# Two-layer hybrid step in float32 on one core: seven products for the latent gate and up projections, and a feed-forward cut in two phases through DRAM

## The chip, the cores and the metric

The kernel runs on one core of one Trainium2 chip (trn2). The metric is the device time of one execution in microseconds; the time of a kernel is the median of its runs. Beside the runs there is one profiled execution, whose records give the rows below. Engines are named as the profile does: PE is TensorE's matmul, PEld its weight load, DVE is VectorE, ACT is ScalarE, POOL is GpSimd, SP is SyncE, which issues the DMAs.

## The reference, cut to what matters

Two trunk layers run over 1024 latent tokens and 256 context tokens with a model width of 1024 and a feed-forward width of 2816. Each layer is a modulated norm, one input projection, three mixers (long convolution, short convolution, attention), an output projection with a gated residual, and then the feed-forward:

```python
x = x + g1 * (y @ P['w_out'][l])
h2 = rmsnorm(x, P['g_norm2'][l]) * (1 + sc2) + sh2
ff = (jax.nn.silu(h2 @ P['w_ff_gate'][l]) * (h2 @ P['w_ff_up'][l])) @ P['w_ff_down'][l]
x = x + g2 * ff
```

`sc2`, `sh2`, `g1` and `g2` are vectors of the width 1024 from a modulation that differs between latent and context tokens. Everything is float32.

## The kernel before

**Products.** Tokens lie along the columns in three chunks (`CH`): two of 512 latent tokens, `ci` 0 and 1, and one of 256 context tokens, `ci` 2. Every float32 operand is held as two float32r parts, hi (a copy on ACT, line 325) and lo (value minus hi, on DVE or POOL, line 326), and each product is three matmuls: hi·hi, hi·lo, lo·hi (`mm3`, line 335). A tile of 128 outputs over the width 1024 is a group of 24 matmuls in one of the eight PSUM banks: three of them belong to the pool `pa`, five to `pb`, given out in turn.

**The feed-forward** (`ffn`, line 1380) goes over 22 tiles f of 128 hidden columns. For each f it loads the gate and up weights (1024 words a partition each), splits them into hi and lo, and `gu` does for the chunks 2, 0, 1 a gate and an up group. ACT puts Silu over the gate (line 1394), DVE multiplies by up from PSUM (1395), POOL splits the product into hi and lo in a ring of two (`ze`, 1396 and 1397). Then `down` takes the hidden tile of the f before: for each chunk and each of 8 output tiles three matmuls, after which DVE adds the result, times g2, to the residual x in SBUF (1411). The last `down` takes two tiles at once, so six matmuls to a group; in layer 1 it also writes the result out (1416). The residual x and both norms' results stay in SBUF all the time.

**What lies ahead of it.** `out_proj` (line 1354) runs over chunk 0, then chunk 1; context went before, inside attention. DVE adds to x (1368), ACT squares (470), POOL sums the squares (473). From the sum `bcast_rstd` makes the reciprocal root: PE (485), a chain of small DVE operations (487, 349 to 356, 494), PE (498). `norm_mod` (504) then scales the eight k tiles on DVE (517), and makes hi and lo: half of the tiles by ACT and DVE (524, 525), half by ACT and POOL (520 to 522). The norm of a chunk is put off by a number of ticks (`soon`, `tick`); that of chunk 1 is made while PE is at the feed-forward's first groups.

**Beside it in layer 0** run the modulation vectors of layer 1: `mod_tiles` (385), three tiles of 1024 words for each f, all through one buffer `rawm`: DMA, DVE (399), POOL (395), ACT (396), then the next tile's DMA.

**Order.** Each engine works through its own queue in order. A planner makes that order when the kernel is built: by program order as priority, taking a later instruction first where its own clock says that the earlier one still waits. A `Mem` object gives every buffer its place in SBUF by the span of program order in which it lives, so two buffers may share a place, and the later one then waits for the readers of the earlier. `open_z` and `close_z` lay out a region anew: `zw` (eight weight buffers) and `ze` during the feed-forward.

## Time and profile before

| | |
|---|---|
| median of 3 runs | 3739.16 us (3738.04 to 3741.91) |
| the profiled execution, its own time | 3742.36 us |
| its span from first to last instruction | 3740.5 us |
| PE busy | 3540.3 us (95%) |
| DVE, POOL, ACT busy | 2226.4 us (60%), 1260.5 us (34%), 1085.3 us (29%) |
| mean granted clock of TensorE | 0.962 |

The page of the profile gives the busy time of each engine, and the span in 40 slices. Matmuls overlap, so a busy PE isn't PE at its peak: how fast it goes is read from how many matmuls it does in a stretch. The chain of waits follows the work back from the last instruction; a piece of it with a count, such as "PE pa L335 x72", is so many matmuls one behind the other, and its time by its count is the pace of one. Granted clock is that of TensorE, 1.00 being 2.4 GHz and 0.5 being 1.2 GHz.

### The profile page before, as it was taken

What the parts mean: (1) busy time and instruction counts of PE and PEld (TensorE: products, weight loads), DVE (VectorE), ACT (ScalarE), POOL (GpSimd) and SP (SyncE); (2) the same over time, 40 slices, a digit from 0 to 9 for tenths busy, and PEclk for the clock granted to TensorE, in tenths of its full rate; (3) what the DMA queues carried; (4) which work ended last, traced back from release to release, by engine and by line L of the source; (5) the groups of instructions that cost most, each with busy time, mean ns of one, the idle gap of its engine ahead of it and who ended that gap; (6) DMA issues with size and microseconds to landing.
All of it is one profiled execution on the core that took longest, in us unless ns stands there. A gap on an engine that the chain in (4) does not pass through costs nothing.

```text
span 3740.5 us, 45633 instructions
## 1 busy us (share of the span) xinstructions
PE 3540.3 (95%) x17792; PEld 2811.7 (75%) x17792; DVE 2226.4 (60%) x3420; ACT 1085.3 (29%) x1955; POOL 1260.5 (34%) x1063
## 2 busy tenths in 40 slices
PE   7899889998999999999999988999899999999999
PEld 4488865555788888888887886655578888888888
DVE  4657577766565666566458757767655445444543
ACT  4422344544331211121124234444533110111010
POOL 3412346665443323332132234556542111111110
PEclk9799889998999999999999999899899999999999
DMA  7611100013322222221122110001331111111111
GB/s 278 230 61 60 38 15 17 21 41 110 103 73 74 79 68 85 74 79 51 46 73 66 62 40 13 11 13 33 117 103 52 34 40 35 46 35 40 34 46 63
DMA packets 84005, 239.23 MB, mean 64 GB/s; under 512 B 8491, under 2 KB 20779, under 8 KB 80588
## 3 DMA queue, kind: packets, MB, share of 16 engines
q1 hardware_dynamic: 83788, 236.30, 19.2%
q8 instruction: 140, 2.29, 0.3%
q14 instruction: 77, 0.63, 0.1%
HBM read 207.89 MB, written 28.38 MB: 63 GB/s over the span
## 4 chain that ended last, share of the span: by engine, by line
PE 81%; DVE 11%; issue 2%; POOL 2%; ACT 2%; DMA 2%; SPq 0%; DVEq 0%; POOLq 0%; ACTq 0%
PE pb L335 40%; PE pa L335 26%; PE st L335 5%; PE y L1166 3%; PE pa L1108 2%; DVE arena L463 1%; PE pa L498 1%; PE pa L1127 1%; DVE arena L741 1%; DVE arena L742 1%; DMA zm<-in_w_modk 1%; PE pa L1110 1%; DVE arena L355 1%; DVE arena L354 1%; POOL arena L1184 1%
## 5 line engine op out<-in xcount | busy, mean ns | idle before, releaser
L335 PE MATMUL pb<-operands,zw 128*128 128x512 f32 (+1 forms) x5592 | 1114.0, 359 | 14.6 <-ACT zw L325 7.3
L335 PEld LDWEIGHTS pb<-operands,zw 128*128 128x128 f32 x5592 | 939.2, 190 | 170.7 <-ACT zw L325 8.1
L335 PE MATMUL pa<-operands,zw 128*128 128x512 f32 (+1 forms) x3240 | 646.7, 359 | 0.2 <-POOL operands L522 0.2
L335 PEld LDWEIGHTS pa<-operands,zw 128*128 128x128 f32 x3240 | 544.3, 189 | 91.8 <-issue 1.2
L325 ACT CAST zw<-arena 128x1024 fp32r<-128x1024 f32 x190 | 199.3, 1050 | 1069.9 <-PE pb L335 571.9
L1396 POOL TENSOR_SCALAR ze<-arena 128x256 fp32r<-128x256 f32 (+1 forms) x132 | 74.9, 568 | 1084.9 <-DVE arena L1395 1084.9
L326 DVE TENSOR_TENSOR zw<-arena,zw 128x1024 fp32r<-128x1024 f32 x174 | 254.9, 1485 | 271.1 <-ACT zw L325 266.8
L335 PE MATMUL pb<-ze,zw 128*128 128x512 f32 (+1 forms) x1980 | 411.7, 358 | 0.0
L1411 DVE SCALAR_TENSOR_TENSOR arena<-pb,arena 128x512 f32<-128x512 f32 (+1 forms) x630 | 386.4, 659 | 11.1 <-PE pb L335 11.1
L335 PEld LDWEIGHTS pb<-ze,zw 128*128 128x128 f32 x1980 | 333.1, 188 | 62.4
L1184 POOL TENSOR_TENSOR arena<-pt,arena 128x512 f32<-128x512 f32 x256 | 338.4, 1322 | 88.0 <-ACT pt L1181 75.2
L335 PE MATMUL st<-operands 97*128 97x512 f32 (+1 forms) x1056 | 326.5, 414 | 7.5 <-ACT pt L1181 7.5
L335 PEld LDWEIGHTS st<-operands 97*128 97x128 f32 x1056 | 193.0, 199 | 109.7 <-issue 68.4
L1181 ACT ACTIVATE pt<-st 128x512 f32<-128x512 f32 (+1 forms) x352 | 201.6, 578 | 227.9 <-PE st L335 216.9
L1395 DVE TENSOR_TENSOR arena<-arena,pb 128x512 f32<-128x512 f32 (+1 forms) x83 | 49.5, 597 | 351.3 <-PE pb L335 344.4
L335 PE MATMUL pa<-ze,zw 128*128 128x512 f32 (+1 forms) x1188 | 254.8, 357 | 0.0
L1411 DVE SCALAR_TENSOR_TENSOR arena<-pa,arena 128x512 f32<-128x512 f32 (+1 forms) x378 | 234.7, 659 | 7.1 <-PE pa L335 7.1
L395 POOL TENSOR_TENSOR arena<-arena 128x1024 f32<-128x1024 f32 x48 | 130.6, 2721 | 296.8 <-DVE arena L399 296.8
L335 PEld LDWEIGHTS pa<-ze,zw 128*128 128x128 f32 x1188 | 200.8, 188 | 37.3
L1166 PE MATMUL y<-pt,kv 128*64 128x512 f32 (+1 forms) x704 | 194.1, 621 | 1.5 <-ACT pt L1181 1.5
L1109 DVE TENSOR_REDUCE arena<-pa 128x1 f32<-128x512 f32 x256 | 168.4, 686 | 36.1 <-PE pa L1108 31.6
L1397 POOL TENSOR_TENSOR ze<-arena,ze 128x256 fp32r<-128x256 f32 (+1 forms) x132 | 148.4, 1124 | 10.9
(240 smaller groups left out, 3992.4 us busy)
## 6 DMA issues: line engine op xcount, KB each, us to landing
zm<-in_w_modk SPq DMA_DIRECT2D x24, 1024.0 KB, 6.3
arena<-in_w_out SPq DMA_DIRECT2D x48, 512.0 KB, 3.5
arena<-in_w_mod SPq DMA_DIRECT2D x48, 512.0 KB, 3.4
arena<-in_w_g SPq DMA_DIRECT2D x44, 512.0 KB, 3.5
arena<-in_w_u SPq DMA_DIRECT2D x44, 512.0 KB, 3.5
arena<-in_w_dn SPq DMA_DIRECT2D x44, 512.0 KB, 4.3
arena<-in_w_in SPq DMA_DIRECT2D x24, 512.0 KB, 3.5
yd<-arena SPq DMA_DIRECT2D x14, 640.0 KB, 3.3
```

The source lines that it names most:

```text
L325: nc.scalar.copy(hi.r, raw.f)
L326: (e or nc.vector).tensor_tensor(out=lo.r, in0=raw.f, in1=hi.f, op=ALU.subtract)
L335: self.nc.tensor.matmul(out, a, b, start=(j == 0), stop=(j == n - 1))
L395: nc.gpsimd.tensor_tensor(out=w.f, in0=w.f, in1=c, op=ALU.mult)
L1108: nc.tensor.matmul(p, q, kh[:96, 512 * c:512 * c + 512], start=True, stop=True)
L1109: v.reduce_max(out=mx[:, t, c:c + 1], in_=p, axis=AX.X)
L1166: ins = nc.tensor.matmul(y[64 * e:64 * e + 64, :n], G["kv"][:, kt0 + k + e, h, 0:64], pts[k + e].f[:, :n], start=(k == 0), stop=(k == nkt ...
L1181: ex = nc.scalar.activation(pt.f[:, :n], st[:, :n], AF.Exp)
L1184: (v if k in KDV else gp).tensor_tensor(out=acc.f[:, :n], in0=pt.f[:, :n], in1=(acc if k > 1 else pts[0]).f[:, :n], op=ALU.add)
L1396: nc.gpsimd.tensor_scalar(out=hi, in0=sg.f, scalar1=1.0, scalar2=0.0, op0=ALU.mult, op1=ALU.add)
L1397: nc.gpsimd.tensor_tensor(out=lo, in0=sg.f, in1=hids[f].f[:, s:s + n], op=ALU.subtract)
L1411: nc.vector.scalar_tensor_tensor(out=xx, in0=p[:, :n], scalar=g2[:, m, q:q + 1], in1=xx, op0=ALU.mult, op1=ALU.add)
```

## The change

For latent tokens the product of a pair of f tiles (256 outputs), the width 1024 and 1024 tokens is seen as 2x2 blocks: A of 128 x 512 weights, B of 512 x 512 activations. Seven block products of 12 matmuls each (4 k tiles, three matmuls) take the place of eight. Sums and differences of weight blocks (S1 to S4) are made on POOL for every pair, those of activation blocks (T1 to T4) once a layer, on DVE and POOL. Part of the additions of results is done by accumulating on in the same PSUM bank after it was read (`mma` with `add`), the rest by DVE. Context tokens keep their plain product (`context`).

The feed-forward is two phases: `gate_up` for all pairs, which writes the hidden values to DRAM (`hd`), then `down`, which reads them back two tiles at a time, splits them, and does six matmuls to a group. The residual x is written to DRAM (`xd`) by `out_proj` and read back when `down` begins. All of norm 2 of chunk 1, and the T forms, are made by `rest` after `out_proj`. The SBUF region of the kernel grows (`NW`, `NZ`), the reserve for software DMA descriptors shrinks (`SCRATCH`). In layer 0 the modulation tiles come five to a pair.

```diff
-NW = 53184
-NSMALL = 960
+NW = 57024
+SCRATCH = 1024
+NSMALL = 736
-NZ = 13312
+NZ = 16896
...
+    def mma(self, out, ops, add):
+        n, j = 3 * len(ops), 0
+        for ah, alo, bh, bl in ops:
+            for a, b in ((ah, bh), (ah, bl), (alo, bh)):
+                self.nc.tensor.matmul(out, a, b, start=(j == 0 and not add), stop=(j == n - 1), skip_group_check=add)
                 j += 1
...
+    def shifted(self, l, k, u):
+        nc = self.nc
+        sh = self.mod[l].v(2)[:, 24 + k, 0:1]
+        hi, lo = self.form(), self.form()
+        nc.scalar.activation(hi.r, u, AF.Identity, bias=sh)
+        nc.vector.scalar_tensor_tensor(out=lo.r, in0=u, scalar=sh, in1=hi.f, op0=ALU.add, op1=ALU.subtract)
+        return hi, lo
+    def forms_first(self, l, us):
+        return {"11": [self.shifted(l, k, us[k]) for k in range(4)], "21": [self.shifted(l, k, us[k]) for k in range(4, 8)]}
...
+    def forms_rest(self, l, u1, u2):
...
+        def split(name, k, t, e):
+            hi, lo = self.form(), self.form()
+            nc.scalar.copy(hi.r, t)
+            e.tensor_tensor(out=lo.r, in0=t, in1=hi.f, op=ALU.subtract)
+            F[name][k] = hi, lo
+        for k in range(4):
+            t2 = self.t5()
+            gp.tensor_tensor(out=u1[k], in0=u2[k], in1=u1[k], op=ALU.subtract)
+            v.scalar_tensor_tensor(out=t2.f, in0=u2[4 + k], scalar=sh[:, 4 + k:5 + k], in1=u1[k], op0=ALU.add,
+                                   op1=ALU.subtract)
+            split("T2", k, t2.f, gp)
+            v.scalar_tensor_tensor(out=u1[4 + k], in0=u1[4 + k], scalar=sh[:, 4 + k:5 + k], in1=t2.f, op0=ALU.add,
+                                   op1=ALU.subtract)
+            t2.free()
+        for k in range(4):
+            split("T1", k, u1[k], v)
+            v.scalar_tensor_tensor(out=u2[k], in0=u2[4 + k], scalar=d[:, k:k + 1], in1=u2[k], op0=ALU.add,
+                                   op1=ALU.subtract)
+        for k in range(4):
+            split("T3", k, u2[k], gp)
+        for k in range(4):
+            F["22"][k] = self.shifted(l, 4 + k, u2[4 + k])
+        for k in range(4):
+            split("T4", k, u1[4 + k], gp)
...
 (out_proj)
+                if m % 2:
+                    nc.sync.dma_start(self.xd[:, m - 1:m + 1, t0:t0 + n],
+                                      x[ci].f[:, n * (m - 1):n * (m + 1)].rearrange("p (k n) -> p k n", n=n))
...
+    def gate_up(self, l, cx, F, rest, extra, ahead):
+        ring = Ring(self.zq, 1024)
+        names = ("11", "12", "S2", "S1", "S3", "21", "22", "S4")
...
+        def prepare():
+            j, w, n = todo.pop(0)
+            src = block(j, w, n)
+            f = ring.get()
+            nc.scalar.copy(f.r[:, 0:512], src)
+            v.tensor_tensor(out=f.r[:, 512:1024], in0=src, in1=f.f[:, 0:512], op=ALU.subtract)
...
+        def free(j, w, *ns):
+            for n in ns:
+                have.pop((j, w, n)).free()
+            need(j, w)
...
+        def result(w, name, src, add=None):
+            B = state["hid"]
+            if w == "g":
+                B[name] = o = self.rings["hb"].get()
+                if add is not None:
+                    v.tensor_tensor(out=o.f, in0=src, in1=add, op=ALU.add)
+                    src = o.f
+                nc.scalar.activation(o.f, src, AF.Silu)
+            elif add is not None:
+                t = self.t5()
+                v.tensor_tensor(out=t.f, in0=src, in1=add, op=ALU.add)
+                gp.tensor_tensor(out=B[name].f, in0=B[name].f, in1=t.f, op=ALU.mult)
+                t.free()
+            else:
+                v.tensor_tensor(out=B[name].f, in0=B[name].f, in1=src, op=ALU.mult)
+        def first(j, w):
+            st = state[w] = dict(X=self.ps(), E=None)
+            (a11,) = need(j, w, "11")
+            self.mma(st["X"], ops(a11, F["11"]), False)
+            st["p1"] = self.t5()
+            nc.scalar.copy(st["p1"].f, st["X"])
+            st["E"] = self.ps()
+            a11, a12 = need(j, w, "11", "12")
+            context(j, w, 0, a11, a12)
+            free(j, w, "11")
+            self.mma(st["X"], ops(a12, F["21"]), True)
+            free(j, w, "12")
+            result(w, "11", st["X"])
+        def second(j, w):
+            st = state[w]
+            p1, Y, Z = st["p1"], self.ps(), self.ps()
+            (f,) = need(j, w, "S2")
+            self.mma(Y, ops(f, F["T2"]), False)
+            free(j, w, "S2")
+            a, b = self.t5(), self.t5()
+            v.tensor_tensor(out=a.f, in0=Y, in1=p1.f, op=ALU.add)
+            (f,) = need(j, w, "S1")
+            self.mma(Z, ops(f, F["T1"]), False)
+            free(j, w, "S1")
+            (f,) = need(j, w, "S3")
+            self.mma(Y, ops(f, F["T3"]), True)
+            free(j, w, "S3")
+            v.tensor_tensor(out=b.f, in0=Y, in1=p1.f, op=ALU.add)
+            a21, a22 = need(j, w, "21", "22")
+            context(j, w, 1, a21, a22)
+            free(j, w, "21")
+            result(w, "c", st["E"])
+            result(w, "22", Z, b.f)
+            b.free()
+            (f,) = need(j, w, "S4")
+            self.mma(Z, ops(f, F["22"]), True)
+            free(j, w, "S4")
+            result(w, "12", Z, a.f)
+            a.free()
+            self.mma(Y, ops(a22, F["T4"]), True)
+            free(j, w, "22")
+            result(w, "21", Y, p1.f)
...
+            if j == 0:
+                need(0, "g")
+                rest()
+                first(0, "g")
+                first(0, "u")
+                second(0, "g")
+                second(0, "u")
+            else:
+                for w in "gu":
+                    first(j, w)
+                    if (j, w) == sets[-1]:
+                        ahead()
+                    second(j, w)
...
+                    nc.sync.dma_start(self.hd[l][:, 2 * j + q, 512 * t:512 * t + 512], b.f)
...
+    def hid_split(self, f):
+        raw = self.hraw.pop(f)
+        for q in range(2):
+            h = self.hids[f + q] = self.rings["hid"].get()
+            for s, n in ((0, 512), (512, 768)):
+                src = raw.f[:, T * q + s:T * q + s + n]
+                self.nc.scalar.copy(h.r[:, s:s + n], src)
+                self.nc.gpsimd.tensor_tensor(out=h.r[:, T + s:T + s + n], in0=src, in1=h.f[:, s:s + n], op=ALU.subtract)
+    def down(self, l, x, early, done):
+        ws = [self.load_split(r, 1024) for r in early]
+        self.hid_load(l, 2)
+        for ci, (s, n) in enumerate(CH):
+            x[ci] = self.al(KD * n)
+            for m in range(0, KD, 2):
+                nc.sync.dma_start(x[ci].f[:, n * m:n * m + 2 * n].rearrange("p (k n) -> p k n", n=n),
+                                  self.xd[:, m:m + 2, s:s + n])
+        for f0 in range(0, NF, 2):
...
+            def ahead():
+                for a, b in F.pop("11") + F.pop("21"):
...
+                self.hid_load(l, 0)
+                self.hid_split(0)
```

`zq`, the ring of weight forms, has five buffers: a product that is done frees one, and the hi and lo of the form five places on are made in it.

## Rows read from the trace of the kernel before

**Rows 1.** Windows: stretch, length; PE, PEld, DVE, ACT, POOL busy; granted clock; DMA.

```profile
1110.00:1900.00 790.00, 790.00 (x4099) 676.77 (x4098) 462.71 (x669) 138.66 (x206) 219.52 (x160) 1.00 0.21 68
2890.00:3730.00 840.00, 840.00 (x4339) 718.56 (x4338) 388.41 (x592) 90.11 (x118) 99.69 (x120) 1.00 0.12 40
```

**Rows 2.** The chain of waits in the feed-forward: start, us, what.

```profile
1203.83 16.32 PE pa L335 x72
...
1400.74 22.10 PE pb L335 x120
...
1429.69 3.50 PE pb L335 x15
...
1567.25 22.10 PE pb L335 x120
...
3717.61 7.00 PE pb L335 x30
```

**Rows 3.** Groups by shape, layer 1's feed-forward (count, busy us, mean ns, idle before).

```profile
L326 DVE TENSOR_TENSOR zw<-arena,zw 128x1024 fp32r<-128x1024 f32 x59 | 70.3, 1220 | 106.1 <-ACT zw L325 106.1
...
L1395 DVE TENSOR_TENSOR arena<-arena,pb 128x512 f32<-128x512 f32 x29 | 20.0, 688 | 205.0 <-PE pb L335 201.2 <-PE pa L335 3.7
...
L325 ACT CAST zw<-arena 128x1024 fp32r<-128x1024 f32 x58 | 61.1, 1054 | 526.7 <-PE pb L335 296.8 <-PE pa L335 155.9 <-issue 74.0
...
L1394 ACT ACTIVATE arena<-pb 128x512 f32<-128x512 f32 x20 | 11.9, 594 | 79.6 <-PE pb L335 79.6
L1397 POOL TENSOR_TENSOR ze<-arena,ze 128x512 fp32r<-128x512 f32 x39 | 50.7, 1300 | 3.3
```

**Rows 4.** The same of layer 0, where modulation tiles run beside.

```profile
L326 DVE TENSOR_TENSOR zw<-arena,zw 128x1024 fp32r<-128x1024 f32 x57 | 103.4, 1841 | 84.1 <-ACT zw L325 84.1
...
L399 DVE SCALAR_TENSOR_TENSOR arena<-arena 128x1024 bf16<-128x1024 f32 x46 | 56.2, 1222 | 84.4 <-DMA arena<-in_w_mod 54.7 <-POOL ze L1397 29.7
...
L395 POOL TENSOR_TENSOR arena<-arena 128x1024 f32<-128x1024 f32 x46 | 124.9, 2715 | 288.2 <-DVE arena L399 288.2
```

**Rows 5.** DVE in order of time, layer 0 (start, us; idle before in brackets).

```profile
1407.64 0.42 DVE L1395 TENSOR_TENSOR arena<-arena,pb 128x256 f32<-128x256 f32 x1
1411.17 1.22 DVE L399 SCALAR_TENSOR_TENSOR arena<-arena 128x1024 bf16<-128x1024 f32 x1 [3.11 <-DMA arena<-in_w_mod]
```

**Rows 6.** Order of time ahead of the feed-forward of layer 1: DVE, ACT, POOL.

```profile
2818.16 0.74 DVE L1368 SCALAR_TENSOR_TENSOR arena<-pb,arena 128x512 f32<-128x512 f32 x1
...
2840.52 0.16 DVE L487 TENSOR_SCALAR arena<-pa 128x4 f32<-128x4 f32 x1
...
2844.29 0.69 DVE L494 TENSOR_TENSOR arena<-arena 128x512 f32<-128x512 f32 x1
2846.28 2.07 DVE L517 SCALAR_TENSOR_TENSOR arena<-arena,pa 128x512 f32<-128x512 f32 x3 [1.30 <-PE pa L498]
2848.26 0.74 DVE L525 SCALAR_TENSOR_TENSOR operands<-arena,operands 128x512 fp32r<-128x512 f32 x1
...
2849.76 1.26 DVE L525 SCALAR_TENSOR_TENSOR operands<-arena,operands 128x512 fp32r<-128x512 f32 x1
...
2819.14 1.28 ACT L1394 ACT_TABLE_LOAD   x1 [0.61 <-PE pb L335]
...
2849.18 1.29 POOL L522 TENSOR_TENSOR operands<-arena,operands 128x512 fp32r<-128x512 f32 x1 [6.60 <-ACT operands L521]
```

**Rows 7.** PE's waits, 1000 to 1100 us; a window as in rows 1.

```profile
PE pb L335 <- POOL operands L522: 1.0, 1, 1.0
PE pa L498 <- DVE arena L494: 0.8, 1, 0.8
...
1016.00:1028.00 12.00, 6.74 (x31) 5.44 (x30) 8.73 (x17) 3.77 (x5) 3.57 (x2) 0.72 0.30 89
```

**Rows 8.** DMAs by kind: count, KB each, us to landing.

```profile
arena<-xd SPq DMA_DIRECT2D x16, 256.0 KB, 3.1
...
arena<-in_xT SPq DMA_DIRECT2D x1, 1024.0 KB, 5.6
```

More of the change, by code (lines that the diff above doesn't have):

```diff
@@ L202, in grow, with shrink @@
         self.count = len(self.bufs)
+    def shrink(self, keep):
+        ks = [k for k in range(self.count) if self.busy[k]]
+        for k in range(self.count):
+            if k not in ks:
+                self.bufs[k].free()
+        self.bufs = [self.bufs[k] for k in ks]
+        for t in keep:
+            t.k = ks.index(t.k)
+        self.busy, self.count, self.at = [True] * len(ks), len(ks), 0
     def close(self):
@@ L372, in consts @@
         self.xd = self.dram.tile([P, KD, T], F32, name="xd")
+        self.hd = [self.dram.tile([P, NF, T], F32, name=f"hd{l}") for l in range(DEPTH)]
         self.kd = [[self.dram.tile([P, 8, 512], F32, name=f"kd{l}{c}") for c in range(2)] for l in range(DEPTH)]
@@ L528, in norm_mod, with norm_raw @@
         return hi, lo
+    def norm_raw(self, l, ci, x, acc):
+        n = CH[ci][1]
+        (r,) = self.bcast_rstd([(acc, 1.0 / D)], n)
+        acc.free()
+        a = self.am[l].f[:, 16:32].rearrange("p (a b) -> p a b", b=2)
+        us = [x[:, k, :] for k in range(KD)]
+        for k in range(KD):
+            self.nc.vector.scalar_tensor_tensor(out=us[k], in0=us[k], scalar=a[:, k, 0:1], in1=r[:, :n], op0=ALU.mult,
+                                                op1=ALU.mult)
+        return us
@@ L1401, in down @@
-        def down(fs, done=None):
-            ws = [self.load_split(self.i["w_dn"][l, f], 1024) for f in fs]
-            for ci in LAST if done and l + 1 < DEPTH else range(3):
+        hids = self.hids
+        ws = [self.load_split(r, 1024) for r in early]
[5 more added lines that the diff above has]
+                                  self.xd[:, m:m + 2, s:s + n])
@@ L1404, in down @@
+        for f0 in range(0, NF, 2):
+            fs, last = (f0, f0 + 1), f0 == NF - 2
+            nws = None
+            for ci in LAST if last and l + 1 < DEPTH else range(3):
                 (s, n), acc = CH[ci], None
@@ L1418, in down @@
                     self.tick()
-                if done:
+                    if ci == 0 and m == 1 and not last:
+                        self.hid_split(f0 + 2)
+                        nws = [self.load_split(self.i["w_dn"][l, f], 1024) for f in (f0 + 2, f0 + 3)]
+                        if f0 + 4 < NF:
+                            self.hid_load(l, f0 + 4)
+                if last:
                     done(ci, acc)
@@ L1551, in run, with rest @@
                 early = ()
-                for ci in cis:
-                    self.soon(NDLY[ci], norm2, ci)
-            self.close_rings("w")
-            self.rings["w"] = Ring(self.zw[4:] + self.zw[:4], 1024)
-            self.rings["hid"] = Ring(self.ze, 2 * T)
+                if cis == (0,):
+                    self.soon(NDLY[0], norm2, 0)
+            self.close_rings("w", "raw")
+            for part in "ab":
+                self.close_z(part)
+                self.open_z(part, "forms")
+            self.fplaces = self.zf + self.zg
+            self.open_rings(raw=("f", 1024, 4), sw=("f", 512, 4))
+            assert not self.late
+            def rest():
+                norm2(1)
+                F.update(self.forms_rest(l, h2[0], h2[1]))
+                x[0].free()
+                x[1].free()
+                self.open_rings(hb=("f", 512, 8))
             extra = None
@@ L1573, in extra @@
                         self.close_rings("rawm")
+            def ahead():
+                for a, b in F.pop("11") + F.pop("21"):
+                    a.free()
+                    b.free()
+                self.open_rings(hrr=("f", 2560, 1), hdr=("r", 2560, 2))
+                self.rings["hid"] = Ring(self.rings["hdr"].bufs, 2 * T)
+                self.rings["hr"] = Ring(self.rings["hrr"].bufs, 2560)
+                self.hraw, self.hids = {}, {}
+                self.hid_load(l, 0)
+                self.hid_split(0)
+            self.gate_up(l, h2[2], F, rest, extra, ahead)
+            early = [self.fetch(self.i["w_dn"][l, f]) for f in range(2)]
+            for hl in (*F.values(), list(zip(*h2[2]))):
+                for a, b in hl:
+                    a.free()
+                    b.free()
+            self.close_rings("sw", "hb")
+            for part in "ab":
+                self.close_z(part)
+            for part in "ab":
+                self.open_z(part, "operands")
+            self.rings["raw"].shrink(early)
+            self.rings["w"] = Ring(self.zw, 1024)
+            self.rings["hid"].grow(self.ze)
+            self.rings["hr"].grow(self.zh)
             def norm1(ci, acc, l=l, h=h):
@@ L1587, in run @@
             self.filler = None
-            self.ffn(l, h2, x, done, extra)
-            self.close_rings("hid", "w")
+            self.down(l, x, early, done)
+            self.close_rings("hrr", "hdr", "w")
+            for name in ("hid", "hr"):
+                self.rings.pop(name)
         self.close_rings("raw", "t5")
```

152 lines of the change are left out of this document (100 added, 52 removed).

## The prediction

> **What bounds the kernel now.** First the windows over the feed-forward of each layer: PE is busy in all of 790.00 and 840.00 us, at a granted clock of 1.00, which is 2.4 GHz, while DVE has 462.71 and 388.41, POOL 219.52 and 99.69, ACT less [rows 1]. A busy PE proves little, so next its pace, from the chain of waits, which in these stretches is nothing but matmuls. 72 matmuls of 512 columns take 16.32 us: 226.7 ns each. The piece of 120 holds 48 of 256 columns beside 72 of 512, so (22.10 - 16.32) / 48 = 120.4 ns. In `down` 15 of 512 columns take 3.50 us, 233.3 ns, and 30 of them in the last `down`, with six to a group and DVE idle half the time, 7.00 us: the same, so DVE doesn't set that pace [rows 2]. The same piece comes again after 1567.25 - 1400.74 = 166.51 us for four tiles f, 41.63 us each [rows 2]. By the paces gate and up take 96 x 226.7 ns + 48 x 120.4 ns = 27.5 us of it, and the rest, 14.1 us, is `down`. There is no slack: the feed-forward, 22 x 41.63 = 916 us in each of two layers, is as long as its matmuls, and one taken out is a gain of its full pace as long as nothing else comes late.
>
> **What is removed.** For a pair of tiles and one of the two weights the latent chunks take 2 x 2 x 24 = 96 matmuls of 512 columns; seven products of 12 are 84. 12 x 226.7 ns = 2.72 us, times 11 pairs, 2 weights and 2 layers (44 sets): **119.7 us** less. Context keeps its 48 matmuls, `down` its count. A set is then 84 x 226.7 + 48 x 120.4 ns = 24.8 us of PE, a pair 49.6.
> *A price from the Trainium skill.* The page TensorE: Matmul & The Clock Gate, section Back-to-back issue gap, gives some 131 ns as the sustained spacing of 512-column matmuls; by it the removed work would be worth 528 x 131 ns = 69 us, and the forecast some 50 us worse. The trace has 226.7 ns here, at full clock [rows 2], so the measurement decides.
>
> **Do the other engines still fit?** Per pair: DVE makes 16 lo parts of 512 words, which I put at half of a 1024 one, 0.61 us as in layer 1 to 0.92 as in layer 0 [rows 3, 4], and 12 additions or multiplications of 0.69 [rows 3]: 18 to 23 us. POOL has 8 weight sums and 3 products at 1.30 [rows 3]: 14.3. ACT has 16 copies at half of 1.05, two of p1 and five Silu of 0.59 [rows 3]: 12.6. Layer 0 adds five modulation tiles: DVE 6.1, POOL 13.6 [rows 4]. All stay under 60% of 49.6. DVE's evictions in `down` halve in number, which gains nothing, as PE's pace there was its own [rows 2].
>
> **Start of the phase.** Before, norm 2 of chunk 1 was hidden by 33 us of context and chunk-0 groups; what PE waited there was 1.0 and 0.8 us in layer 0 [rows 7]. Now PE has only `first` of gate and up ready, 2 x 24 x (226.7 + 120.4) ns = 16.7 us, and then needs T2. In layer 1 PE leaves `out_proj` near 2816.2 (the first context group, 2.9 us, releases ACT at 2819.14), and the last eviction starts at 2818.16, behind norm 2 of chunk 0 [rows 6]. That norm now has eight lo parts on DVE, not four: 4 x 0.74 later, so x is done at 2821.9. Square and sum at ACT's and POOL's prices (0.59 and 1.30 [rows 3]) and PE's reduction give 2824.7; DVE's root chain 4.5 (2840.52 to 2844.98), PE and its hand-over 1.3, eight scalings of 0.66 as 2.07 / 3 shows them with their overlap, 5.3 [rows 6]: 2835.8. T2 is eight DVE operations and four lo parts on POOL. Side by side that is 8 x 0.74 plus 1.9 for the last copy and lo, 7.8; taking turns, 8 x 0.74 + 4 x 1.29 = 11.1 [rows 6]. So T2 ends between 2843.6 and 2846.9; PE would take its last k tile at 2835 or so. A stall of 8 to 11 us, 3 to 5 more for T1, on which DVE spends another 5.9 while PE has 2.7 of work. After a gap the clock is below full for a while: 0.72 over 12 us with some 5 of idle [rows 7]; I add 2.5. Less the 1.5 of before: **+14 a layer, 28 in all**; from 10 (DVE frees x early, as the 1.26 and 0.74 of the same operation show that turns vary [rows 6]) to 44 (all of DVE's and POOL's part in turns).
> The writes of x in `out_proj` are 8 DMAs on SP for the two latent chunks, and 4 for context; each stands ahead of weight fetches on SP's queue and waits for an eviction that PE has just fed. I take 0, at most 5 a layer.
>
> **The seam to `down`.** The first hidden pair is loaded and split inside the last `second`, 16.5 us of PE: a load of 1.3 MB, 5.6 us for 1 MB [rows 8], then four copies and four lo parts, some 6.5 us of POOL [rows 3]. x lies where `hb` lay, whose last slot goes free after an addition, a product and a write: 0.69 + 1.30 [rows 3] + about 3.1, then 3.1 to read x [rows 8], 8.2 us after PE's last product. PE goes on meanwhile through eight banks of 6 x 233.3 ns, 11.2 us: hidden. **+2 a layer, 4 in all** (0 to 20, if the bulk of x, 12 DMAs, comes slower).
>
> **Inside the phase** a set has two narrow places. Y may be added to by S3·T3 only after DVE has read it for `a`, with S1·T1, 2.72 us, as cover. Z may be added to by S4·B22 only after DVE made `b` and the result 22; cover is the context product, 2.89 us. In it DVE has 0.69 + 0.69 and one lo of 0.61 to 0.92: 2.0 to 2.3 us. Where a lo, whose two inputs lie in SBUF, meets POOL, both are longer: a 1024 lo takes 1.22 us in layer 1, and 1.84 in layer 0 with its modulation tiles on POOL [rows 3, 4].
> *The rule of the Trainium skill,* SBUF — State Buffer, section Who interferes with whom: a two-input DVE operation and a POOL operation that reads SBUF lock each other out for a whole instruction. By that a lo could lose a whole 1.30 us more, the stretch would take 3.6 of 2.9 us, and a meeting in every set would cost 44 x 0.7 = 31 us in place of the 12 below; the 1.84 is a mean over meetings and misses, so the rows speak for some loss but not for this size.
> In layer 0 before, with POOL busy 219.52 of 790 us, 28% [rows 1], a lo of 512 words was thus 0.31 longer. In layer 1 POOL will be as busy (14.3 of 49.6): 2.0 + 0.31 still fits, so only odd cases wait, and I take 0.15 us a set, **+3** (0 to 15). In layer 0 it is twice as busy, a lo 0.6 longer and the stretch at its limit: 0.4 us a set, +9; and DVE's queue stands at modulation tiles that came late, 84.4 us over 46 of them, 1.8 each [rows 4], with groups of the feed-forward behind. Before, nothing was urgent behind it. Now a block of w = 3 us (wait and work) that falls ahead of one of the two reads costs on average w²/2 for each place in 24.8 us: 0.36 us, times 48, 17; I take half, as PE gives way once and is then late itself. **+18** for layer 0 (4 to 45).
> The pace of the new products may be that of `down`, where operands lie in a z region: 23 of 56 moving parts lie there, so up to 1518 x 6.7 ns = +10; hidden tiles moved the other way give up to -7. I take +1.
>
> **The sum**, against the profiled execution's own 3742.4: -119.7 + 28 + 4 + 3 + 18 + 1 = -65.7, so 3676.7. The median of the runs lies 3.2 lower than that execution: **3675**, rounded up.
>
> **The rivals.**
> *All is hidden.* Start and seams cost their lower ends, 10 + 0 + 0 + 4 - 7 = 7: 3739 - 113 = 3626, with scatter up to 3645. For it speaks the planner, which fills gaps; against it that T2 stands behind a chain of a length that rows 6 give. Chance 0.13.
> *DVE's queue paces the sets (slower).* In program order the copy and lo for the buffer freed by the context product stand ahead of result 22. They can't begin before that product ends; in that order PE would wait 0.53 + 0.61 (copy, lo), 0.69 for 22, in the up set 0.69 more for the context result, and hand-overs: some 2.4 us in each of 44 sets, 106 us. With start and seam: -119.7 + 106 + 54 = +40, **3780**. It decides the sign from (119.7 - 54) / 44 = 1.5 us a set on. Against it: the order isn't the program's. DVE takes line 1395 of the next tile ahead of a modulation tile, L399, that program order has first [rows 5]; result 22 is ready during the context product and would be taken first. But the planner's clock is not the chip's: the same row shows DVE then standing 3.11 us. Chance 0.12.
> *The change doesn't make products cheaper than what it puts around them.* If the stall at the start, the seam and layer 0 all come out at their upper ends, 44 + 20 + 45 + 10, and layer 1 near its middle, 125 meets 119.7: no change, 3739 to 3745. Chance 0.05.
>
> **How the numbers follow.** Forecast 0.70 (within 3645 to 3725), rivals 0.13, 0.12, 0.05. What differs by under 0.2%, 7.5 us, a measurement of this kernel can't tell from no change. Faster: 0.70 + 0.13 = 0.83; same 0.05; slower 0.12. The range goes from 3630 to 3730: it leaves out a quarter of the first rival, 0.03, and the two others, 0.17, which makes 0.2; the lower bound of the sum, 3626, and the upper ends of all costs together, some 3755, lie just outside.
>
> **What would show it.** Right: a set of 24.8 us in layer 1 with no PE wait over 1 us; between `out_proj` and the first T2 product a PE gap of 8 to 16 us on DVE or POOL of `forms_rest`, with the clock below 1.00 after it; the gap at the seam under 3 us; layer 0's sets longer than layer 1's by some 0.7 us. Wrong: matmuls of the new products off 226.7 ns; PE waits on DVE's reads of Z or Y in every set; a gap at the seam on the DMA of x or of `hd`; a longer stretch outside the feed-forward, which would mean that the new places in SBUF cost something.

## The result and the profile after

The changed kernel takes **3798.57 us** (median of 4 runs, 3794.74 to 3804.2), the kernel before 3740.36 beside it: a ratio of 1.0157, 95% interval 1.014 to 1.0175. It is slower by 58 us, where 65 us of gain were forecast. The profiled execution's span is 3796.3 us; before it was 3740.5. Divided at the ends of the matmuls of `out_proj` and `down`:

| stretch | before, us | after, us | difference |
|---|---|---|---|
| up to the feed-forward of layer 0 | 1037.7 | 1041.8 | +4.1 |
| feed-forward, layer 0 | 921.2 | 1003.4 | **+82.2** |
| from there to the feed-forward of layer 1 | 857.3 | 859.4 | +2.1 |
| feed-forward, layer 1 | 924.3 | 891.7 | **-32.6** |

One change, two layers, two signs. The windows of the kernel after (columns as in [rows 1]) are `gate_up` and `down` of layer 0, then those of layer 1:

```profile
1041.80:1734.45 692.65, 598.52 (x2915) 494.66 (x2914) 339.38 (x454) 214.88 (x377) 334.72 (x186) 0.94 0.31 100
1734.45:2045.20 310.75, 308.06 (x1591) 262.05 (x1590) 207.24 (x310) 60.53 (x89) 93.19 (x58) 1.00 0.26 92
2904.60:3484.00 579.40, 566.62 (x2915) 479.23 (x2914) 257.71 (x349) 170.75 (x279) 190.91 (x138) 0.98 0.23 75
3484.00:3796.30 312.30, 306.77 (x1585) 261.38 (x1583) 201.03 (x287) 47.00 (x60) 76.86 (x41) 1.00 0.27 95
```

`down` is alike in both layers. The two `gate_up` phases hold the same 2915 matmuls, yet layer 0's is 113.25 us longer: 81.35 us in which PE stands (692.65 - 598.52 against 579.40 - 566.62), and 31.9 us in which the same matmuls take longer, at a granted clock of 0.94 instead of 0.98. The other engines are far from full: ACT, the least loaded, works 31% of layer 0's phase, DVE 49%, POOL 48%.

What sets layer 0 apart is the 48 modulation tiles. PE's longest waits from 1125 to 1770 us, 79.2 us with the two left out (line waited for; us, times, longest):

```profile
PE pa L361 <- ACT arena L423: 41.7, 9, 5.4
PE pb L361 <- DVE arena L1588: 18.7, 17, 3.0
PE pa L361 <- ACT arena L1572: 11.1, 8, 1.5
PE pb L361 <- DVE arena L1595: 3.2, 1, 3.2
```

L423 is the sum that ACT makes for a modulation tile, L1588 the sum `a`, L1595 `b`, L1572 the copy of P1. PE reads nothing that L423 writes; one of the nine waits in order of time shows what it stood for. First PE, then DVE, then ACT (start, us; in brackets the idle time before and what ended it):

```profile
1191.89 2.98 PE L361 MATMUL pb<-operands,zq 128*128 128x256 f32 x24
1200.23 5.46 PE L361 MATMUL pa<-operands,zq 128*128 128x512 f32 x12 [5.36 <-ACT arena L423]
1205.48 3.10 PE L361 MATMUL pb<-operands,zq 128*128 128x512 f32 x12
...
1195.28 1.23 DVE L426 SCALAR_TENSOR_TENSOR arena<-arena 128x1024 bf16<-128x1024 f32 x1 [1.63 <-DMA arena<-in_w_mod]
...
1196.43 0.68 DVE L1595 TENSOR_TENSOR arena<-pb,arena 128x512 f32<-128x512 f32 x1
1197.03 2.45 DVE L1514 TENSOR_TENSOR zq<-arena,zq 128x512 fp32r<-128x512 f32 x1
1199.40 0.68 DVE L1556 TENSOR_TENSOR arena<-pa,arena 128x512 f32<-128x512 f32 x1
...
1198.97 1.06 ACT L423 ACTIVATE arena<-arena 128x1024 f32<-128x1024 f32 x1 [5.67 <-POOL arena L422]
```

The product S4·B22 may go on Z only after DVE has read Z for result 22 (L1556). Y was ready when the 24 context matmuls began, at 1191.9. DVE stood 1.63 us for the transfer of a modulation tile, then worked on the tile, and only then made `b`; the lo after it took 2.45 us instead of 0.68, beside POOL's multiply of the same tile; so result 22 ended at 1200.08 and PE resumed at 1200.23. The stand for the tile and the tile itself are 2.8 us of that delay, the longer lo 1.8. ACT's sum ended at the same moment, after 5.67 us at the head of ACT's queue, and the record names it.

The stand costs a second time. From its first matmul to the next group's it is 5.25 us, for twelve matmuls that take 2.81 in layer 1. The window over them (columns as above) shows the granted clock at its lower level, 1.2 GHz, after PE had stood for 5.36 us:

```profile
1200.20:1203.20 3.00, 2.97 (x7) 2.42 (x8) 0.81 (x2) 1.44 (x3) 0.00 (x0) 0.50 0.78 288
```

And it comes back. The same row stands at 1264.51, 1327.40 and 1389.96, one in each pair, some 63 us apart, where layer 1's pairs are 50.51 apart. A lo of 2.25 to 2.45 us stands ahead of result 22 in nine pairs running, each time beside the tile's multiply on POOL. In layer 1 nothing waits between 3029.63 and 3080.14; the chain of waits is matmuls alone (to be read beside [rows 2]):

```profile
3029.63 25.25 PE pb L361 x132
3054.88 11.18 PE pa L361 x60
...
3068.85 5.66 PE pa L361 x36
...
3080.14 25.25 PE pb L361 x132
```

### The profile page after: what moved, and what is told of

Its sections match the earlier page's. It is cut to its first block, busy times and chain, and to the rows that moved or that the text cites. A ratio compares the mean times of both kernels' runs of the same rounds, so it can differ in the third digit from the quotient of the medians.

```text
span 3796.3 us, 45776 instructions
## 1 busy us (share of the span) xinstructions
PE 3470.0 (91%) x17264; PEld 2726.7 (72%) x17264; DVE 2273.9 (60%) x3378; ACT 1284.9 (34%) x2337; POOL 1553.9 (41%) x1145
## 4 chain that ended last, share of the span: by engine, by line
PE 69%; DVE 12%; issue 5%; POOL 5%; DMA 3%; ACT 2%; ACTq 0%; DVEq 0%; POOLq 0%; SPq 0%
PE pb L353 18%; PE pb L361 15%; PE pa L353 14%; PE pa L361 8%; PE st L353 5%; PE y L1263 4%; POOL arena L422 2%; PE pa L1205 2%; DMA arena<-in_w_mod 2%; POOL arena L1506 1%; DVE arena L838 1%; DVE arena L839 1%; PE pa L525 1%; PE pa L1224 1%; DVE arena L380 1%
## 5 line engine op out<-in xcount | busy, mean ns | idle before, releaser
L353 PE MATMUL pb<-operands,zw 128*128 128x512 f32 (+1 forms) x2520 | 516.5, 363 | 6.3 <-DVE zw L344 3.5
L361 PE MATMUL pb<-operands,zq 128*128 128x512 f32 (+1 forms) x2467 | 481.6, 351 | 21.4 <-DVE zq L1514 10.6
L1514 DVE TENSOR_TENSOR zq<-arena,zq 128x512 fp32r<-128x512 f32 x352 | 300.6, 861 | 320.3 <-ACT zq L1513 312.3
L353 PEld LDWEIGHTS pb<-operands,zw 128*128 128x128 f32 x2520 | 429.3, 190 | 80.6 <-DVE zw L344 5.5
L361 PEld LDWEIGHTS pb<-operands,zq 128*128 128x128 f32 x2467 | 397.6, 193 | 88.8 <-DVE zq L1514 12.1
L1506 POOL TENSOR_TENSOR arena<-arena 128x512 f32<-128x512 f32 x176 | 253.0, 1438 | 423.9 <-DVE zq L1514 416.4
L361 PE MATMUL pa<-operands,zq 128*128 128x256 f32 (+1 forms) x1801 | 338.7, 344 | 56.1 <-ACT arena L423 41.7
L353 PE MATMUL pa<-operands,zw 128*128 128x512 f32 (+1 forms) x1704 | 358.8, 368 | 1.2 <-DVE arena L544 0.6
L361 PEld LDWEIGHTS pa<-operands,zq 128*128 128x128 f32 x1801 | 284.1, 196 | 101.9 <-ACT arena L423 43.8
L353 PEld LDWEIGHTS pa<-operands,zw 128*128 128x128 f32 x1704 | 295.6, 191 | 57.1 <-issue 3.9
```

The costliest lines, as they stand in the source:

```text
L353: self.nc.tensor.matmul(out, a, b, start=(j == 0), stop=(j == n - 1))
L361: self.nc.tensor.matmul(out, a, b, start=(j == 0 and not add), stop=(j == n - 1), skip_group_check=add)
L1506: gp.tensor_tensor(out=S[n].f, in0=a, in1=b, op=op)
L1514: v.tensor_tensor(out=f.r[:, 512:1024], in0=src, in1=f.f[:, 0:512], op=ALU.subtract)
```

## The experiments

All ratios are to the kernel before, run beside them on the same chip.

**Theory:** the modulation tiles of layer 0, in the queues of DVE, ACT and POOL, make up the loss. **Rival:** it is the new phase itself (start, seam, Z and Y waits), and layer 1 is merely luckier.

**1. No tiles, in both kernels.** The body of `mod_tiles` is replaced, in the kernel after and in the kernel before:

```diff
-        for j in js:
-            w = self.rings["rawm"].get(1024)
-            ...
+        if 0 in js:
+            nc.vector.memset(self.mod[l].f[:, 0:96], 0.0)
```

> The changed kernel without the 48 modulation tiles of layer 1 (their DMA, DVE, POOL and ACT instructions are left out and the modulation is set to 0, so this part of the computation is missing). Theory A: DVE's and ACT's queues stand at modulation tiles that came late, and the reads of Y and Z stand behind them. Then layer 0's pairs get as short as layer 1's 50.5 us, the 81 us of PE's waits in layer 0's first phase and the 30 us of lowered clock go: 3685 to 3700 us. Theory B: the seven-product sets of layer 0 are slow in themselves (POOL's weight sums, their places in SBUF): 3770 us or more.

> The kernel before without the same 48 modulation tiles (left out in the same way). Theory A: PE never waited in its feed-forward, so nothing is to be had: 3736 to 3743 us. If it gets faster by more than 10 us, the tiles cost something there too, and the gain of the run beside it isn't the change's.

Measured: after without tiles **3685.19** (0.9859, 0.9843 to 0.9874), before without tiles **3740.81** (0.9998, 0.9986 to 1.001), both where theory A had them. The kernel before hid its tiles wholly; in the changed one they cost 113 us. Without them layer 0 runs as layer 1 does; the window from 1125 us:

```profile
1125.00:1700.00 575.00, 573.67 (x2977) 486.82 (x2976) 248.48 (x343) 156.18 (x250) 170.52 (x122) 1.00 0.26 86
```

The rival falls, and the change as such is a gain of 1.4%.

**2. A second tile buffer**, so that a transfer starts before the last tile is done: `open_rings(rawm=("f", 1024, 2))`.

> The changed kernel with two buffers for modulation tiles in place of one, nothing left out: a tile's DMA (3.4 us) no longer waits for the tile before it to leave ACT. Theory A, by way of the DMA: DVE doesn't stand at tiles any more, most of the 81 us and of the clock's loss goes: 3705 to 3740 us. If POOL's and ACT's part of the chain is what counts: 3770 to 3798. Theory B: 3790 to 3800.

Measured **3811.21** (1.0197, 1.0179 to 1.0214): worse by 13 us, and outside all the ranges expected. The run doesn't price DVE's wait for the transfer, because the second buffer took little of it away: from 1125 to 1740 us DVE still stands 37.5 us in 19 waits for a tile, where it stood 49.7 in 30. PE's waits are now 32.6 us for the copy of P1 on ACT, 26.8 for `a`, 21.3 with ACT's tile sum, and DVE's half of a tile takes 1.87 us on the mean instead of 1.47. With two buffers the tiles follow one another sooner; that this is why it got worse is argued, not shown.

**3. Both halves of a tile on DVE**, with the two buffers, so that POOL and ACT have no part in it:

```diff
-                if s:
-                    nc.gpsimd.tensor_tensor(out=w.f, in0=w.f, in1=c, op=ALU.mult)
-                    nc.scalar.activation(w.f, w.f, AF.Copy, accum_out=m[:, j, s:s + 1])
-                else:
-                    scr = self.t5()
+                scr = self.t5()
```

> As the run with two buffers, and both halves of a modulation tile on DVE (two of 1.22 us; no POOL product and no ACT sum). Theory A: nothing of the tiles is left on POOL and ACT, DVE has 1.22 us more a tile and meets no 2.4 us POOL instruction: 3690 to 3715 us. Theory B: 3780 to 3800.

Measured **3754.38** (1.0044, 1.0029 to 1.0059): 44 us of the 113 are back, not the 84 to 109 of theory A; both theories missed. All of PE's waits there but 1.3 us are of one kind:

```profile
PE pb L361 <- ACT arena L1568: 43.4, 10, 5.3
```

ACT's line in order of time says what it is:

```profile
1302.32 0.59 ACT L1568 COPY arena<-pb 128x512 f32<-128x512 f32 x1 [7.41 <-DVE arena L422]
```

L1568 is the copy of P1 (four lines were removed above it), L422 DVE's instruction for a tile. The copy doesn't need the tile's result; it needs its slot. A tile's discarded product goes to a slot of `t5`, the ring that P1 uses next, and DVE runs that tile late.

**4. A buffer of its own for the discarded product**, on the run before (first) and alone in the changed kernel (second):

```diff
-                    scr = self.t5()
+                    scr = self.rings["scr"].get()
```

> The changed kernel with both halves of a modulation tile on DVE and two tile buffers (as the run that gave 3754), and with one thing more: the discarded product of a tile goes to a buffer of its own instead of to a slot of the ring that also holds the copy of P1. Theory A (PE stood once a pair because the copy of P1 had to wait for a slot last written by a modulation tile that DVE runs late): the wait of ACT's copy of P1 goes, 3690 to 3705. Theory B (the five tiles of a pair, bunched, take DVE's time just where the copies' other halves and the sums are needed, whatever slot they write): 3740 to 3755, with PE now waiting for DVE.

> The changed kernel with one thing alone: the discarded product of a modulation tile goes to a buffer of its own; tile buffers, POOL and ACT work as they were. If the shared slot is the largest part of layer 0's loss: 3700 to 3740. If the loss comes from engines that stand at the head of their queue for a tile (DVE for its DMA, ACT for POOL's multiply), which this leaves as it was: 3785 to 3800.

Measured **3714.56** (0.9939, 0.9924 to 0.9954): the wait for P1's copy goes from 43.4 to 0.3 us, 40 us in the total, and the kernel is faster than before: 10 us above theory A's range, as PE now waits 22.8 us for `a`. Alone: **3809.32** (1.0192, 1.0177 to 1.0207), above both ranges, and no gain at all. There the copy of P1 no longer stands for a slot (35.7 us of ACT behind POOL's product, L1562, in the changed kernel, none here), but PE's waits only move: 28.2 us with ACT's tile sum, 20.3 for `a`, 19.6 for the sum of the up set, L1561. So the slot is a cause where DVE holds all of the tile; that in the changed kernel ACT and POOL stand in front of it is argued.

**5. One tile at a time**, at five places of a pair instead of five at its end; first in the changed kernel, then with the cures so far, then with these but a tile's second half on POOL and ACT again:

```diff
             context(j, w, 1, a21, a22)
             free(j, w, "21")
+            if tile and w == "g":
+                tile(j)
...
+                    if tile:
+                        tile(j)
                     second(j, w)
+                    if tile:
+                        tile(j)
```

> The changed kernel with one thing alone: the five modulation tiles of a pair are issued one at a time at five places of the pair (after each half of a set, and once within the set of gate) instead of five in a row at its end. Theory A (five in a row are given precedence over the next pair's work, so DVE, ACT and POOL stand in the chain of transfer, multiply and sum while PE's inputs wait): the chain of one tile has 10 us to itself, 3700 to 3750. Theory B (a single tile already blocks a queue, as ACT's sum waits behind POOL's multiply behind a transfer): 3785 to 3800.

> The run that gave 3714.6 (both halves of a modulation tile on DVE, two tile buffers, the discarded product in a buffer of its own) with one thing more: the tiles are issued one at a time at five places of a pair instead of five in a row. What is left there above the kernel without tiles (3685.2) is 29 us, 22.8 of them PE's wait for DVE's first sum with P1. Theory A (that sum stands behind bunched tiles): 3685 to 3702. Theory B (DVE's time itself, or the transfers, cost it wherever the tiles stand): 3710 to 3725.

> The same three cures (two tile buffers, the discarded product in a buffer of its own, tiles one at a time) with the work of a tile shared as in the changed kernel: one half on DVE, the other a multiply on POOL and a sum on ACT. It differs from the run beside it by that alone. Theory A (ACT at the head of its queue waiting for POOL's multiply is a cause by itself, since P1 and the next weights are copied by ACT): 3735 to 3785. Theory B (only the bunch, the slot and the one buffer did harm): 3690 to 3715.

Measured **3781.92** (1.0121, 1.0105 to 1.0138), 17 us better and just under theory B's range; **3718.65** (0.9943, 0.9928 to 0.9958), no better than without, theory B's range; **3775.95** (1.0095, 1.0079 to 1.0111), theory A's range. The last two differ by the sharing alone, and it costs **57 us**. Their windows from 1125 us, first all on DVE, then shared:

```profile
1125.00:1700.00 575.00, 545.71 (x2774) 459.09 (x2773) 342.19 (x483) 148.68 (x240) 176.46 (x115) 0.98 0.37 120
```

```profile
1125.00:1700.00 575.00, 516.23 (x2548) 432.96 (x2549) 293.72 (x358) 181.12 (x313) 261.89 (x147) 0.94 0.31 101
```

And ACT's wait in the shared one:

```profile
ACT arena L423 <- POOL arena L422: 148.7, 41, 8.7
```

Sharing takes 48 us of work off DVE here, puts 85 on POOL and 32 on ACT, and PE gets less done: a lighter engine, a longer chain. ACT stands up to 8.7 us at the head of its queue for POOL, with the copies of P1 and of the next weights behind. How much of the 57 is that and how much POOL's meetings with DVE I did not separate. Both are there: at least twelve lo parts took 2.3 us or more in the shared run, and none over 1.81 in the other.

The middle run doesn't decide between its theories: DVE's instructions in layer 0's phase have the very order of the run without the five places. A tile on DVE depends on nothing of the set, so the planner takes it as soon as its buffer allows, wherever the code puts it, and all 48 stand between 1087.7 and 1315.3 us, some four of the eleven pairs (the two and a half of the last expectation below were a slip). What is left is then 22.8 us of PE's wait for `a`. One such wait, DVE in order of time and then PE:

```profile
1310.06 1.21 DVE L422 SCALAR_TENSOR_TENSOR arena<-arena 128x1024 bf16<-128x1024 f32 x1
...
1313.59 1.22 DVE L422 SCALAR_TENSOR_TENSOR arena<-arena 128x1024 bf16<-128x1024 f32 x1 [2.31 <-DMA arena<-in_w_mod]
...
1315.34 1.22 DVE L422 SCALAR_TENSOR_TENSOR arena<-arena 128x1024 bf16<-128x1024 f32 x1
...
1316.69 0.68 DVE L1584 TENSOR_TENSOR arena<-pb,arena 128x512 f32<-128x512 f32 x1
...
1317.43 4.63 PE L361 MATMUL pb<-zf,zq 128*128 128x512 f32 x10 [4.15 <-DVE arena L1584]
```

`a` could have run when DVE began to stand for the tile's transfer; it is behind it in the queue.

**6. Where the operands lie.** The ring of weights and most of the forms change regions:

```diff
-                self.zf = take("zf", 14, 512, F32R)
+                self.zq = take("zq", 5, 1024, F32R)
+                self.zf = take("zf", 4, 512, F32R)
...
-            self.zg = take("zg", 9, 512, F32R)
-            self.zq = take("zq", 5, 1024, F32R)
+            self.zg = take("zg", 19, 512, F32R)
```

The rings of weights of `out_proj` and `down` take other slots, so that they don't meet the exchanged tiles.

> The changed kernel with one thing alone: where buffers lie. The ring of weights moves from the right region to the left one (19 of the 23 forms go the other way), so that weights and the moving hidden tiles of the products lie as they do in the second phase, where the trace after shows 0.2267 us a 512-column product. If the place of the operands sets the pace of layer 1's products (0.2325 us, a pair of 50.5 us): a pair of 49.7 to 50.1 us in layer 1, 3780 to 3793 in all. If the place has nothing to do with it: 50.5 us, 3795 to 3800. The modulation tiles stay as they are.

> The run with the three cures and both halves on DVE, and with the ring of weights and the forms in each other's region (a pair of layer 1 took 50.08 us so, 50.51 without). Theory A (the place of the operands is worth 0.43 us a pair in both layers, 22 pairs): 8 to 12 us under the run beside it without the exchange, so 3675 to 3692. Theory B (it changes layer 1's record only, or is lost to another wait): within 3 us of it.

Measured **3798.43** (1.0164, 1.0143 to 1.0184) on the changed kernel, and **3712.58** (0.9925, 0.9907 to 0.9944) beside the 3718.65 without it. In the trace a pair of layer 1 takes 50.08 us (3025.11 to 3075.19) instead of 50.51:

```profile
3025.11 25.04 PE pb L361 x132
3050.15 11.11 PE pa L361 x60
...
3072.47 2.72 PE pa L361 x12
3075.19 4.87 PE pb L361 x30
```

So the place does set part of the pace. In the first total nothing of it is to be seen among waits that vary, so the pair met its range and the total did not. In the second it is 6 us, less than the 8 to 12 expected (3675 to 3692 was set before the run beside it was known): the intervals of the ratios overlap, the runs do not (3709.27 to 3715.5 against 3717.82 to 3719.93).

**7. Tiles tied to a place**, on the second run of experiment 6 and without the five places of experiment 5. The discarded product goes to the buffer that `b` has just left, and the tiles stand behind result 22:

```diff
-            a, b = self.t5(), self.t5()
+            a, b = self.t5(), self.rings["b"].get()
...
             result(w, "22", Z, b.f)
             b.free()
+            if tiles and 1 <= j <= 9:
+                self.mod_tiles(1, [tiles.pop(0) for _ in range(3 if (2 * j + (w == "u")) % 3 else 2)])
...
-                scr = self.rings["scr"].get()
+                scr = self.rings["b"].get()
```

> The run that gave 3712.6 (both halves of a modulation tile on DVE, two tile buffers, the exchange of regions; the one-at-a-time places of the run before had left DVE's order in layer 0 as it was, all tiles in the first two and a half pairs, ahead of the first sum with P1) with one thing changed: the discarded product of a tile goes to the buffer that the second sum with P1 has just left, so a tile can't run before DVE has read that sum for result 22; two or three tiles in each set of nine pairs. Theory A (the remaining 29 us above the kernel without tiles are tiles ahead of the first sum, each standing for its transfer): PE's waits for that sum go, 3676 to 3695. Theory B (a tile costs DVE's time wherever it stands, now ahead of the last results of the set and the copies' other halves): 3703 to 3720.

Measured **3679.8** (3675.5 to 3682.55; 0.9845, 0.9828 to 0.9861): by the ratios some 30 us under the run it builds on (33 by the medians, from two chips) and some 117 under the change as made, faster than the kernel before by 1.55%, and in theory A's range. Layer 0, with all its tiles, now runs pairs of 50.08 us at full clock. The chain of waits:

```profile
1211.47 16.58 PE pb L361 x84
...
1261.55 16.58 PE pb L361 x84
```

And the window:

```profile
1125.00:1700.00 575.00, 572.58 (x2984) 490.34 (x2983) 390.23 (x546) 154.91 (x249) 212.42 (x121) 1.00 0.40 129
```

DVE is busier in it than in any other window shown here, 390.23 of 575 us, and PE waits for it nowhere in that stretch; DVE itself stands 0.4 us for transfers, 8.5 in the run before. What was left here was not DVE's time; it was what stood ahead of what. One thing more changed with the tie: `b` has a buffer of its own and leaves the six slots of `t5` to the others. That was not tried alone.

## Why the prediction failed, step by step

**What bounds the kernel, and the removed work: right.** Without the tiles the change gains 54 to 56 us against its two controls, and layer 1 gains 32.6. `down` keeps its length, 310.75 and 312.30 us with the seam.

**The start: the stall right in size, its path only in part, and the clock behind it too small.** 14 us a layer were forecast, 13 of it a stall before the lowered clock is added. PE's waits from 2904 to 3030 us in the kernel after:

```profile
PE pb L361 <- DVE zq L1514: 5.7, 2, 4.8
PE pa L361 <- POOL zg L601: 3.6, 2, 2.9
PE pb L361 <- ACT arena L1572: 2.5, 1, 2.5
PE pa L512 <- POOL arena L500: 0.5, 1, 0.5
PE pa L361 <- ACT zq L1513: 0.5, 1, 0.5
```

12.8 us (16.1 in layer 0), but in several pieces, not one gap at T2: T2's lo parts on POOL have 3.6 of it, and nearly all the rest are weights and P1's copy on DVE and ACT. That the sum agrees is partly luck. The lowered clock was charged at 2.5 us. The phase of 579.40 us is eleven pairs of 50.51, these 12.8 and another 11.0, and the granted clock was 0.81 over its first 45.4 us, so by an estimate from these the clock cost some four times as much.

**The seam: right.** 1.3 us of PE's waits there in layer 1 (0.53 + 0.80, on DVE's lo of `down`'s first weights), 2 forecast.

**Inside the phase, layer 1: right.** No wait in Z or Y from 3030 us on (the chain above), 3 us forecast.

**Pace: mis-sized.** A pair of 50.51 us holds 168 matmuls of 512 columns and 96 of 256. The pieces of 36 (12 and 24) and 60 (36 and 24) give (11.18 - 5.66) / 24 = 230 ns and (5.66 - 2.76) / 24 = 121 ns; over the pair (50.51 - 11.6) / 168 = 231.6 ns, against 226.7 forecast. The bound that I took, 23 of 56 moving parts at 233.3, assumed that only the moving tile's region matters. The region of the weights counts too: with it exchanged, twelve matmuls with the moving tile in `operands` both times take 2.72 us, 226.7 ns each, where they took 2.81 (the last section has the pairings). It cost (50.51 - 49.65) x 22 = 19 us, where +1 stood, outside the range of -7 to +10.

**The tiles of layer 0: the step that failed.** The sum had +18 for layer 0, +45 at most; it was 113. Three things in it were wrong.
- *A mean over chance meetings.* I let a block of 3 us fall at random ahead of DVE's two reads, w²/2 a place, and halved it. The order of a queue isn't random: the block stands ahead of the same read in every pair, and PE waits for all of it each time, with a lo lengthened by POOL's multiply of the same tile behind it: up to 5.4 us.
- *Only DVE's queue.* The text counted POOL's share of a tile as busy time, under 60% of a pair, and it is; ACT's sums it did not count at all. What it left out is that ACT's sum waits for POOL's multiply, which waits for DVE's half, which waits for the transfer: ACT then stands 236.7 us in 47 waits (L423) with the weight copies and P1 behind it. In the kernel before the same tiles in the same queues cost nothing (experiment 1). Experiment 5 prices the sharing at 57 us. In the nine stands named after ACT's sum what PE resumed on, 0.14 us after its end, was DVE's result 22: POOL's multiply has some 15 us of these 41.7, at up to 1.77 for each lo.
- *No second price for a stand.* The lowered clock was charged at the start, 2.5 us a gap, and not inside layer 0. There it was 31.9 us of the 113, over and above layer 1's.

DVE's lines by shape, layer 0's `gate_up` and then layer 1's, answer [rows 3, 4]:

```profile
L1514 DVE TENSOR_TENSOR zq<-arena,zq 128x512 fp32r<-128x512 f32 x176 | 157.2, 904 | 179.6 <-ACT zq L1513 173.8 <-issue 4.4
L426 DVE SCALAR_TENSOR_TENSOR arena<-arena 128x1024 bf16<-128x1024 f32 x48 | 70.5, 1468 | 49.7 <-DMA arena<-in_w_mod 49.7
...
L1514 DVE TENSOR_TENSOR zq<-arena,zq 128x512 fp32r<-128x512 f32 x176 | 143.4, 818 | 140.7 <-ACT zq L1513 138.4
```

The lo parts came out at 0.90 and 0.82 us, where 0.92 and 0.61 were forecast, and DVE's stands ahead of its half of a tile were no longer than before (49.7 us against 84.4 of all kinds [rows 4, 5]). Layer 1's lo parts were a third longer than forecast and cost PE nothing; what was queued behind was not counted.

**The rivals.** The slower one, DVE's queue pacing the sets at 3780, had the sign, the reads (Z for 22, Y for `a`) and nearly the time. It was given to copies and lo parts in both layers; these hold up nothing in layer 1, so that its time was near is luck, the more as it took 54 us for start and seam where the terms above it make 28 + 4 (3758 with those). The row that I set against the planner, DVE standing 3.11 us for a tile [rows 5], pointed at the cause, and it counted for 0.12. The meeting shown above bears out the rule of the Trainium skill that the prediction weighed (SBUF — State Buffer, section Who interferes with whom): a lo of 512 words took 2.45 us beside POOL's 1024-word multiply and takes 0.68 without, so it lost more than a whole 1.30. POOL's multiply began at 1196.59, 0.44 us ahead of the lo, and ended at 1198.93, 0.55 ahead of the lo's end. What such meetings cost in all was not separated; in layer 1 they cost PE nothing once the pairs run.

**Outside the feed-forward** +6.2 us (4.1 and 2.1), where I had none. PE waits 12.0 us once for the root chain of norm 1, 5.19 before. Six additions on POOL run beside that chain in both kernels, so they don't explain the difference: before, PE still had matmuls for 4 us of the chain, and after it had run out of them, and a 1024-word lo of 1.42 us stands early in the chain. Why the order is so was not tried.

What stays open: how the 57 us of sharing divide between ACT's stand and POOL's meetings; why one more buffer alone made the kernel slower, by 11 and 13 us; why the region's place changes a matmul's pace.

## What to carry to other kernels

Before background work is left in a phase whose inner loop has become tighter, list for each of its instructions what it stands on (a transfer, another engine) and what PE needs from the same queue behind it; a queue with 50% of its time free can still hold PE up in every iteration. Give such work an operand that is free only at the right point of the loop: with all of it on DVE, moving it in the code changed nothing, a shared buffer at the right place gave some 30 us, and one at the wrong place cost 40. When the likely cost of a block is worked out, take its full length times the iterations, not a mean over random meetings, add what the same job's part on another engine does to the instructions behind it, and add the lowered clock behind each stand.

## What the runs showed of the hardware

**A matmul's pace depends on where its operands lie.** In `down` of the kernel after, the weights' ring is the same, and DVE has time. Eighteen matmuls on hidden tiles in `operands` take 4.08 us (226.7 ns each), on tiles in `ze` 4.20 (233.3 ns), by the starts:

```profile
3491.41 4.24 PE L353 MATMUL pa<-operands,zw 128*128 128x512 f32 x18
3495.49 6.96 PE L353 MATMUL pb<-operands,zw 128*128 128x512 f32 x30
...
3519.07 4.36 PE L353 MATMUL pa<-ze,zw 128*128 128x512 f32 x18
3523.27 6.93 PE L353 MATMUL pb<-ze,zw 128*128 128x512 f32 x29
```

It is the pairing that counts. `zw` and `zf` are allotted on the left, `zg` and `ze` on the right; the weights' ring `zq` lies right in the kernel after (first) and left in the exchanged one of experiment 6 (second):

```profile
2963.52 1.52 PE L361 MATMUL pa<-zg,zq 128*128 128x512 f32 x6
2964.88 0.39 PE L361 MATMUL pb<-zg,zq 128*128 128x512 f32 x1
```

```profile
3058.32 1.52 PE L361 MATMUL pa<-zf,zq 128*128 128x512 f32 x6
3059.68 1.57 PE L361 MATMUL pa<-zg,zq 128*128 128x512 f32 x6
3061.09 2.97 PE L361 MATMUL pb<-zg,zq 128*128 128x512 f32 x12
```

With both on one side six matmuls take 1.36 us by the starts, 226.7 ns each; with weights left and `zg` right they take 1.41, 235 ns. Over layer 1's pairs the means are 228.5 (`zg`), 233.7 (`zf`) and 234.4 ns (`operands`) with the weights right, and 233.8, 226.4 and 227.8 with them left. Opposite sides are slow, and `operands` goes with the left. Why is not shown.

**Tiny operations of DVE are not tiny beside POOL.** In the root chain at the end of layer 0, while POOL runs six 512-word additions, 4-word operations take 1.1 us or 0.16 in turns:

```profile
2049.80 1.11 DVE L380 SCALAR_TENSOR_TENSOR arena<-arena 128x4 f32<-128x4 f32 x1
2050.94 0.16 DVE L381 TENSOR_TENSOR arena<-arena 128x4 f32<-128x4 f32 x1
2051.14 1.12 DVE L382 SCALAR_TENSOR_TENSOR arena<-arena 128x4 f32<-128x4 f32 x1
...
2047.28 9.00 POOL L500 TENSOR_TENSOR arena<-arena 128x512 f32<-128x512 f32 x6
```

The same chain in the kernel before has the same turns beside POOL's six additions (1.11 to 1.22 and 0.16 us). In the chain of [rows 6], which the forecast took at 4.5 us, POOL ran one subtraction, from 2841.29, and one of the 4-word operations took 1.13 us. So a chain's length depends on what POOL does beside it.
